# Pinning the order of the casts and subtractions that make the weight forms of a fast matrix product

## The chip, the cores and the metric

The kernel runs on one core of one Trainium2 chip. The metric is the device time of one execution in microseconds (us), the median of several runs. The engines are TensorE (PE, with its weight loads shown as PEld), VectorE (DVE), ScalarE (ACT), GpSimd (POOL) and SyncE (SP). SP, ACT and POOL issue the DMAs.

## The reference

One layer of a decoder trunk on 512 tokens of width 2048, in float32: a norm, a combined projection, two kinds of attention, an output projection, and then the gated MLP in which the change lies:

```python
D_MODEL = 2048; SEQ = 512; D_FF = 5632
def conv_ffn(h, w_up, conv_w, conv_b, w_down):
    u, g = jnp.split(h @ w_up, 2, axis=-1)
    u = lax.conv_general_dilated(
        u, conv_w[:, None, :], window_strides=(1,), padding=((CONV_WIDTH - 1, 0),),
        dimension_numbers=('NWC', 'WIO', 'NWC'), feature_group_count=D_FF) + conv_b
    return (jax.nn.silu(u) * g) @ w_down

x = x + g2 * conv_ffn(h, w_up[l], conv_w[l], conv_b[l], w_down[l])
return rms_norm(x, norm_final)
```

The first product is `h @ w_up`, the second is the one with `w_down` (5632 x 2048).

## The kernel before

A float32 operand is split into two parts that PE takes at its faster rate: a high part, made by a cast on ACT (L215), and a low part, the operand less the high part, made by a subtraction on DVE (L218). `split_to` makes both, and each product of two matrices is three matmuls: high by high, high by low, low by high.

The second product is done block by block with a scheme that needs seven products instead of eight for a matrix cut into 2 x 2 blocks. The 44 feature tiles make five groups of eight and a last group of four, which is done plainly at the end (`Kept`, `last_slots`). A group has two passes, one for each half of the output columns, so there are ten passes, `n` = 0 to 9. In a pass there are seven products, `pos` = 0 to 6, each in two halves of the depth, `p` = 0 and 1. One `pos` and `p` is a slot: 12 matmuls of 128x512 into the output tile `p` (class `Down`).

A pass works on four raw weight blocks a, b, c, d of 128x1024 for each `p`. For `p` = 0 they lie in tiles of their own (`qa`, `qb`, `qc`, `qd`); for `p` = 1 they lie in two shared tiles, `rawca` and `rawbd`. Block a of passes 2, 4, 6 and 8 lies in `rawa`. `dn_cut` makes the weight form of a slot. It splits a block (`cut`, into one of four tiles `wd` that are used in turn), combines blocks in place on DVE for a later position (L1285 c - a, L1290 s = d - c, L1296 s - a, L1308 b - s; s is `qs` or `rawst`), and calls `dn_load`, which has SP load a block of the next pass over the one just used (L1278).

The activations need forms as well, `af`, made once for a group by `act_form` out of the tiles `stage`: four positions of them are made in the second pass of the group before, positions 3 to 6, and three in the first pass of the group itself, positions 0 to 2. They take the subtractions L1261 to L1266 and further splits.

`drive` runs over the slots and calls `split` three slots ahead of the matmuls. Results leave PSUM by a copy on ACT (L1375) and are added up in memory by DMAs of POOL (`total`, L1320).

This is the order in which the program is recorded, and it is not the order in which the engines run it. A scheduler sets the order of every engine's queue from priorities and from its own estimate of when operands are ready. An engine then works through its queue in that order. `tc.keep_in_program_order` adds an order edge from the instruction recorded just before on the same engine, so that the scheduler can't put the pinned instruction ahead of it. Before the change the loads L1278, the sums of POOL and some casts of other parts are pinned; `split_to` and `cut` have an argument `keep` that pins the cast alone.

The first product runs up to about 1640 us of the span (tiles `ux`, `uy`, `uz`); its last slots overlap with the first of the second one. The convolution's vectors `y`, the sums `ut` and `gt` and the modulation row `mod` of its last unit are still on DVE and ACT then.

Of the kernel before, what the change touches and what calls it, by code (L numbers as in the profile page):

```python
# [11 lines left out]
OP = mybir.AluOpType  # L12
# [21 lines left out]
def hybrid_trunk(ctx, tc, xT, cT, wm, bm, nrm, wik, wiq, wi1, sinks, kvn, wuk, wuv, rel, onehot,  # L34
                 wo, wup, cw, cb, wdn, out):
    nc = tc.nc
    act, dve, pe, pool, sp = nc.scalar, nc.vector, nc.tensor, nc.gpsimd, nc.sync
# [176 lines left out]
    def split_to(hi_t, lo_t, full, keep=False):  # L214
        hi = act.copy(hi_t, full)  # L215
        if keep:
            tc.keep_in_program_order(hi)
        dve.tensor_tensor(lo_t, full, hi_t.bitcast(F32), OP.subtract)  # L218
# [809 lines left out]
    def cut(x, name, keep=False):  # L1028

        w = env["px0"].tile([P, 2, 1024], F32R, tag=f"x2_{cut_turn[0] % 4}", name=f"w{name}")  # L1030
        cut_turn[0] += 1
        split_to(w[:, 0], w[:, 1], x, keep)
        return w[:, 0], w[:, 1]
# [201 lines left out]
    def raw_place(tag, p, name, n):  # L1235
        if tag == "a" and n > 1 and n % 2 == 0:
            return down_t["a2"][:, p]
        return down_t[tag] if p else fr_tile(tag, name)
# [32 lines left out]
    def dn_load(n, p, tag):  # L1271
        if n >= 2 * GROUPS:
            return
        g, c = divmod(n, 2)
        t = dn_raw[n, p, tag] = raw_place(tag, p, f"q{tag}{n}_{p}", n)
        k, dq = {"a": (0, c), "b": (1, c), "c": (0, 2 + c), "d": (1, 2 + c)}[tag]
        tc.keep_in_program_order(
            sp.dma_start(t.rearrange("p (a b) -> p a b", a=2), wdn[2 * g + k, dq][:, 2 * p:2 * p + 2]))  # L1278

    def dn_cut(n, pos, p):  # L1280
        a, b, c, d = [dn_raw[n, p, t] for t in "abcd"]
        name = f"d{n}_{pos}_{p}"
        if pos == 0:
            w = cut(a, name)
            dve.tensor_tensor(c, c, a, OP.subtract)  # L1285
            return w
        if pos == 1:
            w = cut(c, name)
            s = dn_raw[n, p, "s"] = raw_place("s", p, f"qs{n}_{p}", n)
            dve.tensor_tensor(s, d, c, OP.subtract)  # L1290
            dn_load(n + 1, p, "c")
            return w
        s = dn_raw[n, p, "s"]
        if pos == 2:
            w = cut(s, name)
            dve.tensor_tensor(a, s, a, OP.subtract)  # L1296
            return w
        if pos == 3:
            w = cut(d, name)
            dn_load(n + 1, p, "d")  # L1300
            return w
        if pos == 4:
            w = cut(a, name)
            dn_load(n + 2 if n else 1, p, "a")
            return w
        if pos == 5:
            w = cut(b, name)
            dve.tensor_tensor(b, b, s, OP.subtract)  # L1308
            return w
        w = cut(b, name)  # L1310
        dn_load(n + 1, p, "b")
        return w

# [17 lines left out]
    class Down:  # L1331
# [9 lines left out]
        def split(self):  # L1341
            if self.w is None:
                g, odd = divmod(self.n, 2)
                if self.p and odd and self.pos > 2 and g + 1 < GROUPS:
                    act_form(g + 1, self.pos - 3)
                elif self.p and not odd and self.pos < 3 and g:
                    act_form(g, self.pos + 4)
                self.w = dn_cut(self.n, self.pos, self.p)
# [458 lines left out]
```

## Time and profile before

| | |
|---|---|
| median of 3 runs | 2110.59 us (2108.61 to 2114.93) |
| the profiled execution | 2113.66 us, span 2111.9 us |
| mean granted TensorE clock | 0.995 |
| DVE busy, whole span | 1711.7 us (81%) |
| ACT busy, whole span | 1181.4 us (56%) |
| second product | 1639.8 to 2043.5 us, 1680 matmuls of 128x512 |

The profile is of one execution. A row of a timeline has the start in us from the start of the span, the length, the engine and line, what is written and read, the count, and in brackets the idle time of the engine before it with what ended it. Buffer numbers are left out of names. A matmul's recorded length overlaps with the next one's, since matmuls are pipelined.

### The profile page before, as it was taken

How to read it: one execution, taken by the hardware profiler on the slowest of the kernel's cores; microseconds unless marked ns; L12 is line 12 of the kernel's file. 1: busy time of each engine (PE TensorE's matmuls, PEld its weight loads, DVE VectorE, ACT ScalarE, POOL GpSimd, SP SyncE). 2: the span in 40 equal slices, each digit the busy share in tenths (PEclk: the TensorE clock that was granted, in tenths of full speed). 3: DMA queues.
4: the chain of work that ended last, by engine and by line, in shares of the span. 5: the costliest groups of instructions: out<-in, count | busy, mean ns of one | idle time of the engine just before them, and what ended most of it. 6: DMA issues, size and time to landing. Idle time of an engine off the chain costs nothing.

```text
span 2111.9 us, 30184 instructions
## 1 busy us (share of the span) xinstructions
PE 2061.8 (98%) x11050; PEld 1705.7 (81%) x11050; DVE 1711.7 (81%) x2484; ACT 1181.4 (56%) x1950; POOL 287.8 (14%) x432
## 2 busy tenths in 40 slices
PE   8999999999999999999999999999999999999997
PEld 4677877777888888888888888888888787778787
DVE  2887889877868778888888888888888987877867
ACT  4324887677833265555455455555555665665655
POOL 0000000011033200121111111111111111111120
PEclk9999999999999999999999999999999999999999
DMA  9883122567699824887777877787787779989992
GB/s 387 271 278 128 56 74 67 163 212 221 198 349 331 264 88 136 214 217 215 207 215 211 214 215 210 213 221 203 211 223 202 248 236 238 239 212 264 211 237 91
DMA packets 148341, 442.98 MB, mean 210 GB/s; under 512 B 17375, under 2 KB 31855, under 8 KB 141408
## 3 DMA queue, kind: packets, MB, share of 16 engines
q1 hardware_dynamic: 89856, 278.13, 39.4%
q0 software_dynamic: 48832, 145.62, 30.2%
q10 hardware_dynamic: 9504, 17.31, 2.2%
q8 instruction: 86, 1.41, 0.3%
q14 instruction: 63, 0.52, 0.1%
HBM read 366.40 MB, written 58.46 MB: 201 GB/s over the span
## 4 chain that ended last, share of the span: by engine, by line
PE 75%; DVE 11%; DMA 5%; issue 4%; ACT 4%; POOL 0%; SPq 0%; DVEq 0%; ACTq 0%; POOLq 0%
PE ux L53 22%; PE uy L53 11%; PE p L53 9%; PE uz L53 5%; PE qip L53 4%; DVE wd L218 2%; DMA rawca<-in_wdn_dram 2%; DVE af L218 1%; PE ckv L53 1%; DMA mraw<-in_wm_dram 1%; PE mrow L53 1%; PE o L53 1%; DVE wk L688 1%; PE mps L53 1%; DVE top L685 1%
## 5 line engine op out<-in xcount | busy, mean ns | idle before, releaser
L53 PE MATMUL p<-wd,af 128*128 128x512 f32 x1680 | 385.7, 390 | 13.3 <-DVE wd L218 12.8
L53 PEld LDWEIGHTS p<-wd,af 128*128 128x128 f32 x1680 | 314.1, 188 | 84.4 <-DVE wd L218 18.6
L53 PE MATMUL ux<-t_up,wu 128*128 128x512 f32 (+1 forms) x1968 | 368.5, 340 | 1.7 <-DVE gt L1176 1.7
L53 PEld LDWEIGHTS ux<-t_up,wu 128*128 128x128 f32 x1968 | 301.0, 188 | 49.4 <-DVE gt L1176 3.7
L53 PE MATMUL uy<-h,wu 128*128 128x512 f32 (+1 forms) x1312 | 244.2, 339 | 0.0
L53 PEld LDWEIGHTS uy<-h,wu 128*128 128x128 f32 x1312 | 200.7, 188 | 30.1
L231 DVE SCALAR_TENSOR_TENSOR macc<-mraw,c_sb,macc 128x512 f32<-128x512 f32 x240 | 179.5, 748 | 11.3 <-DMA mraw<-in_wm_dram 9.2
L218 DVE TENSOR_TENSOR wu<-ra,wu 128x1024 fp32r<-128x1024 f32 x82 | 100.2, 1222 | 62.0 <-ACT wu L215 62.0
L53 PE MATMUL ux<-h,wu 128*128 128x512 f32 (+1 forms) x656 | 128.6, 339 | 0.0
L215 ACT CAST wu<-rb 128x1024 fp32r<-128x1024 f32 x82 | 86.3, 1053 | 64.5 <-issue 31.6
L53 PE MATMUL uz<-h,wu 128*128 128x512 f32 (+1 forms) x656 | 122.3, 339 | 0.0
L215 ACT CAST wu<-ra 128x1024 fp32r<-128x1024 f32 x82 | 86.1, 1051 | 56.9 <-PE uy L53 49.9
L215 ACT CAST wu<-rs 128x1024 fp32r<-128x1024 f32 x41 | 43.2, 1053 | 129.4 <-DVE rs L1102 81.3
L53 PEld LDWEIGHTS ux<-h,wu 128*128 128x128 f32 x656 | 100.5, 188 | 15.2
L53 PEld LDWEIGHTS uz<-h,wu 128*128 128x128 f32 x656 | 100.5, 188 | 15.1
L218 DVE TENSOR_TENSOR wu<-rb,wu 128x1024 fp32r<-128x1024 f32 x82 | 100.2, 1222 | 8.6 <-ACT wu L215 8.6
L1375 ACT COPY ev<-p 128x512 f32<-128x512 f32 x140 | 81.3, 584 | 25.1 <-PE p L53 21.2
L1320 POOL DMA_DIRECT2D total<-ev x62 | 52.7, 855 | 296.1 <-ACT ev L1375 255.4
L218 DVE TENSOR_TENSOR wu<-rd,wu 128x1024 fp32r<-128x1024 f32 x41 | 50.2, 1225 | 52.3 <-ACT wu L215 52.3
L215 ACT CAST wu<-rd 128x1024 fp32r<-128x1024 f32 x41 | 43.1, 1052 | 69.9 <-PE ux L53 68.2
L1177 POOL DMA_DIRECT2D gt<-gt x41 | 35.2, 860 | 337.7 <-DVE gt L1176 283.1
L1074 POOL DMA_DIRECT2D re<-in_wup_dram x40 | 34.5, 862 | 311.1 <-DMA re<-in_wup_dram 271.4
(1697 smaller groups left out, 4590.8 us busy)
## 6 DMA issues: line engine op xcount, KB each, us to landing
mraw<-in_wm_dram POOLq DMA_DIRECT2D x160, 256.0 KB, 5.8
total<-ev POOLq DMA_DIRECT2D x70, 512.0 KB, 8.0
mraw<-in_wm_dram SPq DMA_DIRECT2D x32, 1024.0 KB
mraw<-in_wm_dram POOLq DMA_DIRECT2D x48, 512.0 KB, 6.4
ra<-in_wup_dram SPq DMA_DIRECT2D x41, 512.0 KB
rc<-in_wup_dram SPq DMA_DIRECT2D x41, 512.0 KB
rb<-in_wup_dram SPq DMA_DIRECT2D x41, 512.0 KB
rd<-in_wup_dram SPq DMA_DIRECT2D x41, 512.0 KB
```

Source lines behind the costliest of these rows:

```text
L53: return self.to.matmul(out, w, x, **kw)
L215: hi = act.copy(hi_t, full)
L218: dve.tensor_tensor(lo_t, full, hi_t.bitcast(F32), OP.subtract)
L231: tc.keep_in_program_order(dve.scalar_tensor_tensor(acc, t, cact[:, kt:kt + 1], acc, OP.mult, OP.add))
L685: dve.max(top[b][:, r], cur[b])
L688: dve.match_replace(wk[b], top[b][:, r], cur[b], -3e38)
L1074: tc.keep_in_program_order(pool.dma_start(duo_raw[f, "e"], duo_part(f, "d"), accum_op=OP.add))
L1177: tc.keep_in_program_order(pool.dma_start(g[:, 1], g[:, 2], accum_op=OP.add))
L1320: tc.keep_in_program_order(pool.dma_start(to, x, accum_op=OP.add))
L1375: act.copy(e[:, b], ps)
```

## The change

In `dn_cut` every `cut` gets `keep` = True, so that each cast of a weight form is pinned behind the instruction recorded before it on ACT; and the four in-place subtractions L1285, L1290, L1296 and L1308 are pinned behind the instruction recorded before them on DVE. The low-part subtraction L218 inside `split_to` isn't pinned itself. No instruction is added or removed.

```diff
         if pos == 0:
-            w = cut(a, name)
-            dve.tensor_tensor(c, c, a, OP.subtract)
+            w = cut(a, name, True)
+            tc.keep_in_program_order(dve.tensor_tensor(c, c, a, OP.subtract))
             return w
         if pos == 1:
-            w = cut(c, name)
+            w = cut(c, name, True)
             s = dn_raw[n, p, "s"] = raw_place("s", p, f"qs{n}_{p}", n)
-            dve.tensor_tensor(s, d, c, OP.subtract)
+            tc.keep_in_program_order(dve.tensor_tensor(s, d, c, OP.subtract))
             dn_load(n + 1, p, "c")
             return w
         s = dn_raw[n, p, "s"]
         if pos == 2:
-            w = cut(s, name)
-            dve.tensor_tensor(a, s, a, OP.subtract)
+            w = cut(s, name, True)
+            tc.keep_in_program_order(dve.tensor_tensor(a, s, a, OP.subtract))
             return w
         if pos == 3:
-            w = cut(d, name)
+            w = cut(d, name, True)
             dn_load(n + 1, p, "d")
             return w
         if pos == 4:
-            w = cut(a, name)
+            w = cut(a, name, True)
             dn_load(n + 2 if n else 1, p, "a")
             return w
         if pos == 5:
-            w = cut(b, name)
-            dve.tensor_tensor(b, b, s, OP.subtract)
+            w = cut(b, name, True)
+            tc.keep_in_program_order(dve.tensor_tensor(b, b, s, OP.subtract))
             return w
-        w = cut(b, name)
+        w = cut(b, name, True)
         dn_load(n + 1, p, "b")
         return w
```

How the queues change is shown at three places. In the names a weight form is `wd_`, its position, its `p` and a number of the tile; an activation form is `af_` with its position.

The first is DVE's queue in pass 3, positions 1 to 3. Tiles 16138 to 16215 belong to pass 3; `qc_0_16140` and the `rawca` that is combined with `rawa` are block c of pass 4.

```order
-L218 TENSOR_TENSOR wd_0_1_16116<-rawca,wd_0_1_16116 128x1024
+L218 TENSOR_TENSOR wd_2_1_16194<-rawst,wd_2_1_16194 128x1024
 L1296 TENSOR_TENSOR rawca<-rawst,rawca 128x1024
-L218 TENSOR_TENSOR wd_1_0_16135<-qc_0_15877,wd_1_0_16135 128x1024
-L218 TENSOR_TENSOR wd_1_1_16156<-rawca,wd_1_1_16156 128x1024
-L1285 TENSOR_TENSOR qc_0_16140<-qc_0_16140,rawa_15613 128x1024
-L218 TENSOR_TENSOR wd_2_0_16178<-qs_0_16138,wd_2_0_16178 128x1024
-L218 TENSOR_TENSOR wd_2_1_16194<-rawst,wd_2_1_16194 128x1024
-L1285 TENSOR_TENSOR rawca<-rawca,rawa_15613 128x1024
 L218 TENSOR_TENSOR wd_3_0_16215<-qd_0_15959,wd_3_0_16215 128x1024
```

Before, the two subtractions L1285 for pass 4 stood among the low parts of positions 1 and 2 of pass 3; now they are gone from here, and L1296 for `rawca` stands behind the low part of its own position.

The second is the same queue at the end of pass 3 and the start of pass 4, where `wd_0_0_16374` is the first form of pass 4.

```order
-L1290 TENSOR_TENSOR qs_0_16415<-qd_0_16218,qc_0_16140 128x1024
 L218 TENSOR_TENSOR wd_6_1_16353<-rawbd,wd_6_1_16353 128x1024
 L218 TENSOR_TENSOR wd_0_0_16374<-rawa_15613,wd_0_0_16374 128x1024
-L1290 TENSOR_TENSOR rawst<-rawbd,rawca 128x1024
+L1285 TENSOR_TENSOR qc_0_16140<-qc_0_16140,rawa_15613 128x1024
 L218 TENSOR_TENSOR af_4_16390<-stage_15230,af_4_16390 128x1024
 L218 TENSOR_TENSOR wd_0_1_16393<-rawa_15613,wd_0_1_16393 128x1024
+L1285 TENSOR_TENSOR rawca<-rawca,rawa_15613 128x1024
+L218 TENSOR_TENSOR wd_1_0_16412<-qc_0_16140,wd_1_0_16412 128x1024
+L1290 TENSOR_TENSOR qs_0_16415<-qd_0_16218,qc_0_16140 128x1024
 L218 TENSOR_TENSOR af_4_16390<-stage_15231,af_4_16390 128x1024
```

The subtractions L1285 and L1290 for pass 4 now stand in pass 4, each behind the low part that is recorded before it. The other passes change in the same way.

The third is ACT's queue at the handover from the first product, where `rawst` and `stage` hold activations for pass 0.

```order
 L215 CAST wd_0_0_15266<-qa_0_15179 128x1024
-L215 CAST wd_0_1_15298<-rawca 128x1024
 L215 CAST af_0_15202<-stage_01_15048 128x1024
 L1041 ACTIVATE y_15258<-y_15258 128x512
 L215 CAST af_15291<-stage_11_15050 128x1024
 L1044 DMA actd_1646<-y_15258 128x512
+L215 CAST af_2_15294<-rawst 128x1024
+L215 CAST wd_0_1_15298<-rawca 128x1024
 L215 CAST wd_1_0_15302<-qc_0_15103 128x1024
-L215 CAST af_2_15294<-rawst 128x1024
 L1184 COPY gt_15264<-ux_15128 128x256
```

The cast of the second weight form of pass 0 has moved behind five rows, the last of them the cast of activation form 2. Later on ACT the cast of `wd_4_1` moves behind that of `wd_5_0` in pass 0, and behind that of an activation form in the odd passes 1, 3, 5 and 7; its other rows stay, but for a few evacuations in pass 0. On SP one load of `rawa` moves ahead of a load of `rawca`; POOL's queue stays as it was. PE's queue changes in pass 0 alone, where the matmuls on the high and the low parts of the first forms are put in another order.

## The prediction, made before the result was known

> **What bounds the kernel now.** I read the page first. TensorE (PE) is busy for 98% of the span, so only the gaps that it still has can be won, and I looked for those of the second product (output tile `p`, weight forms `wd`, activation forms `af`).
>
> ```profile
> span 2111.9 us, 30184 instructions
> PE 2061.8 (98%) x11050; PEld 1705.7 (81%) x11050; DVE 1711.7 (81%) x2484; ACT 1181.4 (56%) x1950; POOL 287.8 (14%) x432
> L53 PE MATMUL p<-wd,af 128*128 128x512 f32 x1680 | 385.7, 390 | 13.3 <-DVE wd L218 12.8
> ```
>
> The 1680 matmuls of this product stood idle for 13.3 us, 12.8 of it behind VectorE (DVE) writing a low weight part. The timeline of PE alone (start, length, what, and in brackets the idle time before it) gives the places.
>
> ```profile
> 1643.34 3.09 PE L53 MATMUL ux<-t_up,wu 128*128 128x512 f32 x16 [1.72 <-DVE gt L1176]
> ...
> 1649.09 8.64 PE L53 MATMUL p<-wd,af 128*128 128x512 f32 x36 [1.02 <-DVE wd L218]
> 1658.22 0.50 PE L53 MATMUL p<-wd,af 128*128 128x512 f32 x1 [0.49 <-ACT ev L1375]
> 1659.10 37.96 PE L53 MATMUL p<-wd,af 128*128 128x512 f32 x166 [0.38 <-DVE wd L218]
> 1698.38 81.89 PE L53 MATMUL p<-wd,af 128*128 128x512 f32 x360 [1.32 <-DVE wd L218]
> 1781.86 13.94 PE L53 MATMUL p<-wd,af 128*128 128x512 f32 x60 [1.58 <-DVE wd L218]
> 1796.62 25.01 PE L53 MATMUL p<-wd,af 128*128 128x512 f32 x108 [0.83 <-DVE wd L218]
> 1822.54 38.39 PE L53 MATMUL p<-wd,af 128*128 128x512 f32 x168 [0.91 <-DVE wd L218]
> 1862.60 13.90 PE L53 MATMUL p<-wd,af 128*128 128x512 f32 x60 [1.67 <-DVE wd L218]
> 1877.35 25.01 PE L53 MATMUL p<-wd,af 128*128 128x512 f32 x108 [0.85 <-DVE wd L218]
> 1903.25 51.97 PE L53 MATMUL p<-wd,af 128*128 128x512 f32 x228 [0.89 <-DVE wd L218]
> 1955.99 25.02 PE L53 MATMUL p<-wd,af 128*128 128x512 f32 x108 [0.77 <-DVE wd L218]
> 1983.57 59.91 PE L53 MATMUL p<-wd,af 128*128 128x512 f32 x263 [2.55 <-DVE wd L218]
> ...
> 2098.77 0.35 PE L53 MATMUL rs_1s<-ones,tail 128*128 128x1 f32 x2 [0.22 <-DVE tail L1479]
> ```
>
> There are three small gaps at the handover from the first product, nine from 1698 on, and then none until 2098.77, after the last product: whatever the second product saves, the end should come earlier by as much. Why DVE is late shows in its own timeline ahead of the gap at 1781.86.
>
> ```profile
> 1771.66 1.23 DVE L1285 TENSOR_TENSOR qc<-qc,rawa 128x1024 f32<-128x1024 f32 x1 [5.58 <-DMA qc<-in_wdn_dram]
> 1772.80 1.22 DVE L218 TENSOR_TENSOR wd<-qs,wd 128x1024 fp32r<-128x1024 f32 x1
> ...
> 1779.44 1.23 DVE L1285 TENSOR_TENSOR rawca<-rawca,rawa 128x1024 f32<-128x1024 f32 x1 [4.29 <-issue]
> 1780.58 1.22 DVE L218 TENSOR_TENSOR wd<-qd,wd 128x1024 fp32r<-128x1024 f32 x1
> ```
>
> Both L1285 subtractions belong to the next pass and read blocks that are still in flight. The queue of SP shows when those loads went out, and ScalarE (ACT) shows that the hi part of the form was long there:
>
> ```profile
> 1763.39 0.33 SPq L1278 DMA_DIRECT2D qc<-in_wdn_dram  x1
> 1766.11 0.33 SPq L1278 DMA_DIRECT2D rawca<-in_wdn_dram  x1
> ```
> ```profile
> 1771.93 1.06 ACT L215 CAST wd<-qd 128x1024 fp32r<-128x1024 f32 x1 [1.19 <-PE p L53]
> ```
>
> The loads take 8.3 us (1763.39 to 1771.66) and at most 13.3 us (1766.11 to 1779.44). The cast for wd<-qd was done at 1772.99; its DVE half waited in line behind L1285 until 1780.58 and ended at 1781.80; PE started at 1781.86. So the last wait is a load, held at the head of DVE's queue. The view of waits over 1655 to 2044 (total us, times, longest) says that this is the pattern:
>
> ```profile
> ACT wd L215 <- PE p L53: 69.1, 70, 4.0
> DVE qc L1285 <- DMA qc<-in_wdn_dram: 23.2, 5, 6.8
> ACT af L215 <- DVE stage L1262: 17.8, 4, 6.0
> DVE rawca L1285 <- issue: 15.7, 4, 5.2
> DVE qs L1290 <- DMA qd<-in_wdn_dram: 8.2, 3, 3.1
> DVE rawca L1285 <- DMA rawca<-in_wdn_dram: 7.7, 3, 4.0
> ```
>
> The four DVE rows make 54.8 us of waiting; PE feels only what outlasts its lead.
>
> **The change, part by part.** Nothing is added or removed: 70 pairs of pass and position keep their casts, subtractions and loads.
>
> *The subtractions of DVE.* In the steady passes L1285, L1290 and L1296 move back to the pass that uses them. L1285 for the first half goes about twelve slots later (a slot is 12 matmuls of one weight form). A slot is 2.72 us: row 1698.38 holds 360 matmuls, (81.89 - 0.39) / 359 = 0.227 us each. Twelve slots are 33 us behind the load's issue, for a load that needs 8.3 to 13.3; L1290 comes ten slots (27 us) after its load of `qd`. So the 54.8 us of waits should go, and with them the nine gaps. A break costs the idle time plus what a matmul's record overhangs its successor, 0.39 - 0.227 = 0.16 us:
>
> 1.32 + 1.58 + 0.83 + 0.91 + 1.67 + 0.85 + 0.89 + 0.77 + 2.55 = 11.37 us; with 9 x 0.16 = 1.47, 12.8 us.
>
> Two kinds are in this sum. 1698, 1781, 1822, 1862, 1903 and 1983 follow a late L1285 at once. 1796 and 1877 come 14.8 us after the gap ahead of them, while DVE works off its backlog without a pause, and I take 1955 to be of that kind; with no stall there is no backlog.
>
> *What is late next: DVE in the crowded stretch.* From position 4 of an odd pass to position 2 of the next, DVE must also split the activation forms. In the changed order 30 instructions stand there for 12 slots: 30 x 1.135 us (1771.66 to 1772.80, back to back) = 34.0 us against 32.7 of PE. Before, two of them (L1285) had been done ahead of it. The excess of 1.4 us comes out of the lead: a cast may start when the slot four back has ended, three slots (8.2 us) before its use, and cast plus subtraction take 1.05 + 1.22, so 5.9 us are free. Walking the changed queues through with these durations, the tightest form is done 4 us before PE wants it. Cost taken: nothing. If the cover were gone, PE would wait for what exceeds 5.9 us.
>
> *The casts of ACT.* Most keep their rows. In odd passes the cast for `wd_4_1` now stands behind the form cast that waits for L1262 (17.8 us over four times, longest 6.0, because DVE was late); queued behind it are `wd_5_0` and an evacuation. With DVE on time L1262 ends 0.6 us into a slot and the subtraction of `wd_4_1` is done 4 us ahead of use. Nothing.
>
> *The handover.* Here ACT casts `af_2` before `wd_0_1`, and DVE takes L1180, L1266 and the `af_2` subtraction first.
>
> ```profile
> 1644.53 1.06 ACT L215 CAST af<-rawst 128x1024 fp32r<-128x1024 f32 x1 [0.71 <-DVE rawst L1264]
> ```
> ```profile
> 1644.41 1.22 DVE L218 TENSOR_TENSOR wd<-rawca,wd 128x1024 fp32r<-128x1024 f32 x1
> ...
> 1647.82 1.22 DVE L218 TENSOR_TENSOR wd<-qc,wd 128x1024 fp32r<-128x1024 f32 x1
> ...
> 1657.83 1.22 DVE L218 TENSOR_TENSOR wd<-qs,wd 128x1024 fp32r<-128x1024 f32 x1
> ```
>
> The low half of `wd_0_1` ends at 1648.5 instead of 1645.6, that of `wd_1_0` at 1650.8 instead of 1649.0. PE is reordered to match (hi products first). Following it matmul by matmul, the first 51 are issued by 1659.2; before, the 52nd started at 1659.10 after its gaps. I take 0, between a loss of 2.9 us (the delay of `wd_0_1` in full) and a gain of 1.9 (1.02 + 0.49 + 0.38 all gone).
>
> *SP's queue* at one place: the first `rawa` load of pass 2 is put ahead of `rawca` of pass 1 and of the two `stage` loads.
>
> ```profile
> 1668.98 0.33 SPq L1278 DMA_DIRECT2D rawca<-in_wdn_dram  x1
> ...
> 1678.58 0.80 SPq L1278 DMA_DIRECT2D rawa<-in_wdn_dram  x2
> ```
> ```profile
> 1667.81 0.33 ACTq L1044 DMA_DIRECT2D actd<-y  x1
> ut<-ut POOLq DMA_DIRECT2D x41, 256.0 KB, 3.4
> ```
>
> It waits for the first product's buffers to be free. Their last store, also 256 KB, goes out at 1667.81; at the 3.4 us that a transfer of that size takes on POOL's queue (an estimate) it lands at 1671.2. So `rawca` goes out about 2 us late, and its user has 5.9 us of lead. 0, at worst 3. POOL's queue is unchanged, its transfers following PE's pace.
>
> The sum: 12.8 us off the profiled execution. That one took 2113.66 us for a span of 2111.9, 3.1 above the median 2110.59; taken off the median, **2097.8 us**, say 2098 (0.6%). A change below 0.3% (6.3 us) can't be told from none here.
>
> **A rule against it.** PE also waits behind buffers: in the first of the wait rows the casts themselves wait 69.1 us for PE to free one of four weight tiles. If the gaps came from that, order would not help. The Trainium skill (Perfetto Trace Analysis, Optimization Strategy) says that a gap repeating on the engine that should be saturated can mean that there isn't enough SBUF or PSUM for the next tile. By that rule the time would stay at 2110.6. The rows speak against it: at 1781.86 the cast had been over for 8.9 us when PE went on, so a tile was there.
>
> **The rivals.**
> 1. *Forecast*: all nine gaps go, 2098. Chance 0.60.
> 2. *The backlog gaps stay*, since DVE has more to do in the crowded stretch: 1796, 1877 and 1955 keep 0.83 + 0.85 + 0.77 + 3 x 0.16 = 2.9 us: 2100.7. 0.13.
> 3. *The handover pays* its bound of 2.9 us: 2100.7, with rival 2 2103.6. 0.12.
> 4. *No change*: the gaps are for want of tiles, or the loads are late anyway. For the second the DMA share would have to be at its end:
>
> ```profile
> 1640.00:2044.00 404.00, 389.01 (x1702) 317.08 (x1701) 321.68 (x287) 252.16 (x323) 60.09 (x75) 1.00 0.89 234
> ```
>
>    The last two numbers are the share, 0.89, and 234 GB/s. The same transfers in 391 us make 0.92: room, though little. Time 2110.6, chance 0.08. By the Trainium skill (Perfetto Trace Analysis, Identifying the Most-Contended Engine) bandwidth and not occupancy tells whether DMA binds; the row gives both, and no run so far decides between them.
> 5. *Slower: DVE and ACT in lockstep in the crowded stretch.* Nine times there a cast waits for a DVE result and a DVE subtraction for that cast. If none of the nine casts were covered by another DVE instruction, DVE would idle 9 x 1.05 = 9.5 us, and 34.0 + 9.5 - 32.7 - 5.9 = 4.9 us would reach PE, in four stretches 19.6: 2110.6 + 19.6 - 12.8 = 2117.4. It decides as soon as more than four of nine are bare (4.5 us), and beats the gain at about eight. Against it: in the changed order at least one other subtraction (1.135 us) stands between each such pair. 0.07.
>
> That the change does nothing is ruled out by the order: DVE's queue is another one in every pass.
>
> **Numbers.** Faster by over 0.3% (under 2104.3) hold rivals 1 to 3: 0.85, less 0.02 for several small losses at once: 0.83. Within: 0.10. Slower: 0.07. The range reaches down to all gaps and the handover's 1.9 gone, with the scatter of the runs (some 2 us), 2094, and up to rivals 2 and 3 together, 2104.
>
> **What would show it.** Right: no idle DVE time ahead of L1285, PE without gaps from 1660 to the last product, the handover's length as before, DVE's idle time now behind casts of `wd`. Wrong: gaps <-DVE wd around positions 4 to 2 of odd to even passes (rivals 2, 5), DMA waits in front of L1290 or a cast (4), a gap over 2 us before 1660 (3).

## The result, and the profile after

The changed kernel takes 2098.86 us (median of 4, 2098.56 to 2101.0), the kernel before 2112.76 (median of 4, 2108.61 to 2115.35): a ratio of 0.9937, with a 95% interval from 0.9921 to 0.9953. The forecast was 2098. The profiled execution of the changed kernel took 2099.02 us, for a span of 2097.3.

The page of the changed kernel, in the rows that were shown of the kernel before:

```profile
span 2097.3 us, 30196 instructions
PE 2056.4 (98%) x11050; PEld 1705.2 (81%) x11050; DVE 1714.3 (82%) x2484; ACT 1183.9 (56%) x1950; POOL 287.8 (14%) x432
L53 PE MATMUL p<-wd,af 128*128 128x512 f32 x1680 | 382.2, 389 | 1.7 <-DVE wd L218 1.1
```

The idle time of the second product's matmuls fell from 13.3 to 1.7 us. Their busy time fell too, by 3.5 us, though they are as many; this is taken up below. The timeline of PE from the end of the first product (start, length, what, idle time before it):

```profile
1642.54 3.09 PE L53 MATMUL ux<-t_up,wu 128*128 128x512 f32 x16 [1.95 <-DVE gt L1176]
...
1646.72 0.73 PE L53 MATMUL p<-wd,af 128*128 128x512 f32 x2 [0.44 <-ACT wd L215]
1647.75 1.43 PE L53 MATMUL p<-wd,af 128*128 128x512 f32 x5 [0.30 <-DVE wd L218]
1650.02 377.94 PE L53 MATMUL p<-wd,af 128*128 128x512 f32 x1666 [0.84 <-DVE wd L218]
...
2044.34 0.44 PE L57 MATMUL cT<-identr,ct 128*128 128x128 f32 x2 [0.92 <-DMA ct<-total]
```

From 1650.02 on, 1666 matmuls run as one piece: all nine gaps are gone. Small ones are left at the handover, and a new one of 0.92 us stands in the tail, ahead of the transposes `cT`. The view of waits over 1655 to 2032 (total us, times, longest) says what the other engines now wait for:

```profile
DVE wd L218 <- ACT wd L215: 53.5, 66, 3.0
...
ACT wd L215 <- PE p L53: 36.9, 45, 1.1
...
ACT af L215 <- DVE stage L1262: 3.4, 4, 0.9
```

No row of DVE waiting for a load is left; the 54.8 us are gone. Part of that idle time is still there, but now behind casts, whose forms PE needs later: 53.5 us, against the row of the kernel before (1655 to 2044)

```profile
DVE wd L218 <- ACT wd L215: 20.8, 22, 1.5
```

Where the span's 14.6 us come from, by these rows and those of before:

- Ahead of the handover, where nothing was changed, the last row of `ux` stands 0.80 us earlier. That is taken as scatter.
- The handover: the run from 1650.02 begins with the 15th matmul of the product. A matmul takes (377.94 - 0.39) / 1665 = 0.2268 us on average. By the starts of the single matmuls in the trace the 52nd starts at 1658.56; before, at 1659.10. That is 0.54 earlier, so 0.26 was lost against the 0.80.
- From the 52nd matmul to the end of the last: before, 1983.57 + 59.91 - 1659.10 = 384.38 us; now 1650.02 + 377.94 - 1658.56 = 369.40. 14.98 us are won here.
- The tail gives back 0.92. In all, 0.80 - 0.26 + 14.98 - 0.92 = 14.6.

### The profile page after: what moved, and what is told of

Its sections match the earlier page's. It is cut to its first block, busy times and chain, and to the rows that moved or that the text cites. A ratio compares the mean times of both kernels' runs of the same rounds, so it can differ in the third digit from the quotient of the medians.

```text
span 2097.3 us, 30196 instructions
## 1 busy us (share of the span) xinstructions
PE 2056.4 (98%) x11050; PEld 1705.2 (81%) x11050; DVE 1714.3 (82%) x2484; ACT 1183.9 (56%) x1950; POOL 287.8 (14%) x432
## 4 chain that ended last, share of the span: by engine, by line
PE 81%; DVE 6%; issue 5%; DMA 4%; ACT 3%; POOL 0%; SPq 0%; DVEq 0%; POOLq 0%; ACTq 0%
PE ux L53 22%; PE p L53 17%; PE uy L53 11%; PE uz L53 5%; PE qip L53 4%; DMA mraw<-in_wm_dram 2%; DMA total<-ev 1%; PE ckv L53 1%; PE mrow L53 1%; DVE wk L688 1%; DVE top L685 1%; PE mps L53 1%; DVE sa L803 1%; PE o L53 1%; PE wo2ps L53 1%
## 5 line engine op out<-in xcount | busy, mean ns | idle before, releaser
L218 DVE TENSOR_TENSOR wu<-ra,wu 128x1024 fp32r<-128x1024 f32 x82 | 100.1, 1221 | 61.6 <-ACT wu L215 61.6
L218 DVE TENSOR_TENSOR wu<-rb,wu 128x1024 fp32r<-128x1024 f32 x82 | 100.1, 1221 | 8.2 <-ACT wu L215 8.2
L218 DVE TENSOR_TENSOR wu<-rd,wu 128x1024 fp32r<-128x1024 f32 x41 | 50.2, 1225 | 51.8 <-ACT wu L215 51.8
```

## The experiments

**Which pins do it.** Two theories. The one of the prediction: what cost time was L1285 waiting in DVE's queue for a load in flight, so its pins alone bring the whole gain. The rival: the casts come in a better order, or it takes all pins together. The first kernel has the four pins of DVE alone (L1285 and L1290 are shown, L1296 and L1308 are edited in the same way).

```
-            dve.tensor_tensor(c, c, a, OP.subtract)
+            tc.keep_in_program_order(dve.tensor_tensor(c, c, a, OP.subtract))
...
-            dve.tensor_tensor(s, d, c, OP.subtract)
+            tc.keep_in_program_order(dve.tensor_tensor(s, d, c, OP.subtract))
...
```

> Only the four in-place subtractions on DVE are pinned, the casts on ACT are not. Theory (subtractions of the next pass stood early in DVE's queue and waited there for loads in flight): the nine gaps of PE after 1660 us are gone, time 2099 within 3 us, ratio to the kernel before 0.9935. Rival (the pinned casts bring the gain): within 3 us of the kernel before, about 2111.

Measured: 2096.78 us, ratio 0.9928 (0.9913 to 0.9942): the whole gain. The second has the seven pins of the casts alone (one of the seven is shown).

```
-            w = cut(a, name)
+            w = cut(a, name, True)
...
```

> Only the casts on ACT are pinned, DVE's subtractions are free and L1285, L1290 stay early as before. Theory: the nine gaps stay, about 2111 (within 3 us of the kernel before), ratio 1.000. Rival (the casts bring the gain): about 2099.

Measured: 2113.06 us, ratio 1.0002 (0.999 to 1.0014): nothing. Its page has the gaps, its waits have the loads, as before:

```profile
L53 PE MATMUL p<-wd,af 128*128 128x512 f32 x1680 | 387.6, 392 | 12.8 <-DVE wd L218 12.2
```
```profile
DVE qc L1285 <- DMA qc<-in_wdn_dram: 16.4, 4, 6.1
DVE rawca L1285 <- issue: 12.2, 4, 3.6
```

The third pins one line, L1285; the queues of PE, ACT, SP and POOL are then the same as before, and the handover with them.

```
-            dve.tensor_tensor(c, c, a, OP.subtract)
+            tc.keep_in_program_order(dve.tensor_tensor(c, c, a, OP.subtract))
```

> One of the eleven pins: L1285 alone. The queues of PE, ACT, SP and POOL are row for row those of the kernel before; on DVE L1285 moves back into its own pass and pulls L1290 along, since that reads its result. Theory: all of the gain, 2099 to 2101, no wait of L1285 for a load, no gap of PE after 1660. Rival (the gain needs the casts, or the new order on PE or SP at the handover): no gain, or less than half of it, 2105 to 2111.

Measured: 2099.34 us, ratio 0.9937 (0.9923 to 0.9951), and one piece of 1629 matmuls behind the handover:

```profile
1658.60 369.54 PE L53 MATMUL p<-wd,af 128*128 128x512 f32 x1629 [0.40 <-DVE wd L218]
```

One pin is enough. It moves L1285, and L1290, which reads its result, moves along; what L1290's 8.2 us of waits for `qd` cost by themselves was not tried. The fourth kernel is the changed one with that pin taken off and the other ten left.

```
-            tc.keep_in_program_order(dve.tensor_tensor(c, c, a, OP.subtract))
+            dve.tensor_tensor(c, c, a, OP.subtract)
```

> Ten of the eleven pins, L1285 is free: the scheduler puts it one to three rows later than before (behind wd_2_0 and wd_3_0 of the pass ahead), still about nine slots early. Theory: the wait of L1285 for its load shrinks by one or two slots (2.7 to 5.4 us of 5 to 7), so that some of the gaps stay: 2101 to 2108. Rival (the other pins bring the gain): 2099, no gaps.

Measured: 2102.82 us, ratio 0.9953 (0.994 to 0.9965). The other pins alone push L1285 one to three rows back, and the loads have landed for the most part; two rows of waits are left, 12.4 + 4.3 = 16.7 us in place of the 46.6 of L1285 before, and 2.8 us of idle time at the matmuls. These pins bring 9.8 us, the pin at L1285 alone 13.3: most of the gain comes as soon as L1285 stands a few rows further back.

```profile
DVE rawca L1285 <- DMA rawca<-in_wdn_dram: 12.4, 5, 3.5
DVE qc L1285 <- DMA qc<-in_wdn_dram: 4.3, 3, 3.5
```
```profile
L53 PE MATMUL p<-wd,af 128*128 128x512 f32 x1680 | 384.3, 390 | 2.8 <-DVE wd L218 2.2
```

**The early place, or the load?** Moving L1285 changes two things, where DVE spends its time and what it waits for. This kernel keeps the early place and takes the loads away.

```
             dve.tensor_tensor(s, d, c, OP.subtract)
-            dn_load(n + 1, p, "c")
+            dn_raw[n + 1, p, "c"] = c
```

> Before with no pin, but the 18 loads of block c after pass 0 left out: L1285 then works again and again on the block that lies there (another sum is computed). On DVE L1285 stands as early as before, in three places one row earlier still. Theory (what costs is a load in flight at the head of DVE's queue, not the early place): no DMA wait ahead of L1285 or L1290, no gap of PE from 1660 to the last product, 2098 to 2100 us. Rival (the early place costs by itself, because each L1285 puts the low parts behind it back by 1.135 us into a crowded queue): the gaps stay, 2108 to 2113.

Measured: 2100.22 us (2095.46 to 2101.39), ratio 0.995 (0.993 to 0.997). L1285 stands as early as before, and PE runs through:

```profile
1655.13 369.58 PE L53 MATMUL p<-wd,af 128*128 128x512 f32 x1629 [0.42 <-DVE wd L218]
```

So it was the loads. Two short waits of L1285 for `rawa`, 2.9 and 0.4 us in pass 1, are left, though none was expected; PE does not feel them. This also tells what stood behind a row that the profile had left without a cause: the 15.7 us of `rawca L1285 <- issue` before are gone with the loads of block c, though those of `rawa`, which it reads too in two of the four places, are still there.

**How much lead there is in the crowded stretch.** The prediction took nothing for DVE's 34.0 us of work in 32.7, because the tightest form would be done 4 us early. These kernels are the changed one with more work in the second half of that stretch, positions 0 to 2 of the even passes, and look for the end of the lead there. Three more subtractions a stretch:

```
                 self.w = dn_cut(self.n, self.pos, self.p)
+                for _ in range(1 * (self.p and self.n in (2, 4, 6, 8) and self.pos < 3)):
+                    tc.keep_in_program_order(dve.tensor_tensor(*[down_t["spare"]] * 3, OP.subtract))
```

> As the kernel with six, but three in a stretch, one behind the second form of each position: 3.4 us. Theory (some 4 us of lead): nothing, 2098 to 2100. Rival A: 4 x 3.4 = 13.6, 2112. Rival B: nothing; the pair of runs tells theory from both.

Measured: 2099.54 us, ratio 0.9943 (0.9922 to 0.9964): free. Six more (without the condition on `self.p`):

> The changed kernel with six more DVE subtractions of 128x1024 (of one unused tile from itself, 1.135 us each) in each of four crowded stretches, one behind every form of positions 0 to 2 of passes 2, 4, 6 and 8: 6.8 us of DVE work a stretch. Theory (the tightest form is done some 4 us before PE wants it): what exceeds the lead reaches PE, 6.8 - 4 = 2.8 us and the 0.16 of a break, in four stretches 12: 2109 to 2112. Rival A (DVE is at its end there already): all of it, 4 x 6.8 = 27: 2126. Rival B (much more lead than worked out): nothing, 2099.

Measured: 2106.67 us, ratio 0.9974 (0.9964 to 0.9984). Against the 2099.54 of the kernel with three more that is 7.1 us, 1.8 in each stretch: between the rivals, but less than the 12 expected. PE's timeline around the first stretch:

```profile
1649.42 88.17 PE L53 MATMUL p<-wd,af 128*128 128x512 f32 x386 [0.85 <-DVE wd L218]
1738.24 2.83 PE L53 MATMUL p<-wd,af 128*128 128x512 f32 x11 [0.64 <-DVE wd L218]
1741.64 73.96 PE L53 MATMUL p<-wd,af 128*128 128x512 f32 x325 [0.57 <-DVE wd L218]
```

The place is right: the gap ahead of 1738.24 ends with the low part of the second form of position 2, in DVE's timeline of that kernel

```profile
1736.95 1.23 DVE L218 TENSOR_TENSOR wd<-rawst,wd 128x1024 fp32r<-128x1024 f32 x1
```

which ends at 1738.18. The lead in the changed kernel can be read directly. This form is the 34th of the product; PE comes to it with matmul 397, in the trace at 1736.76. DVE's timeline of the changed kernel has its low part in the row

```profile
1731.53 1.22 DVE L218 TENSOR_TENSOR wd<-rawst,wd 128x1024 fp32r<-128x1024 f32 x1
```

which ends at 1732.75, 4.0 us before, and the other forms of positions 0 to 3 are done 4.2 to 5.6 before. So the 4 us were right for this part of the stretch (for the part ahead of it they were not, as the next section shows), and the expected price was still wrong. PE's queue in the kernel with six more says why:

```
 L53 MATMUL p_1_0_15902<-wd_2_1_15940,af_2_15770 128x512 [waits Activation_49]
 L53 MATMUL p_1_1_15903<-wd_2_1_15940,af_2_15770 128x512
 L53 MATMUL p_5_0_15945<-wd_3_0_15962,af_2_15770 128x512 [waits Activation_49]
 L53 MATMUL p_5_1_15946<-wd_3_0_15962,af_2_15770 128x512 [waits Activation_49]
 L53 MATMUL p_1_0_15902<-wd_2_1_15940,af_2_15770 128x512 [waits DVE_49]
```

In the changed kernel the second matmul of the form waits for DVE; here three more matmuls, which need only high parts, stand ahead of that wait, as the scheduler has laid out PE's queue anew. Four of 0.2268 are 0.9 us, so the lead is 4.9; five added subtractions stand ahead of this form, 5 x 1.135 = 5.7 us; 0.8 is short, and the row shows 0.64 + 0.16 for the break. The sixth stands ahead of the next form and makes the second gap, 0.57 + 0.16. Twelve more a stretch (a 2 in place of the 1):

> As the kernel with six more DVE subtractions in each crowded stretch, but two behind every form: 13.6 us a stretch. Six cost 7.1 us in four stretches, so about 6.8 - 1.8 = 5.0 us of a stretch were covered. If the lead is one cover used once a stretch: 4 x (13.6 - 5.0) = 34, 2134. Rival (DVE catches up between the forms, so that the cover counts again): under 2125.

Measured: 2131.4 us (2130.02 to 2135.6), ratio 1.01 (1.0084 to 1.0116), where the changed kernel took 2098.04 on the same chip: 33.4 us, 8.3 a stretch, so 13.6 - 8.3 = 5.3 were covered. The lead is used up once a stretch; past it DVE's work costs nearly its full time: 6.8 us more a stretch than with six subtractions cost 6.6 us more.

**Tiles.** The rival of the prediction that gaps are for want of weight tiles is tried by taking one of the four away from pass 2 on, and making forms two slots ahead instead of three (three further calls of `drive` are edited like the one shown).

```
-        w = env["px0"].tile([P, 2, 1024], F32R, tag=f"x2_{cut_turn[0] % 4}", name=f"w{name}")
+        w = env["px0"].tile([P, 2, 1024], F32R, tag=f"x2_{(cut_turn[0] + 2) % 3 if name > 'd2' and name[0] == 'd' else cut_turn[0] % 4}", name=f"w{name}")
...
-        drive(slots, at, at + 28)
+        drive(slots, at, at + 28, ahead=2)
...
```

> The changed kernel with three weight tiles in turn instead of four from pass 2 on, and forms made two slots ahead instead of three: each cast has 2.72 us less. Theory (a lead of 4 us in the tightest place, and tiles were never what lacked): 4 - 2.7 = 1.3 us are left, 2098 to 2102. Rival (weight tiles bound the casts, which wait 36.9 us for PE to free one): a gap of up to 2.7 us at each of the four crowded stretches or more often, 2110 and above.

Measured: 2099.5 us, ratio 0.9947 (0.9928 to 0.9965). The casts wait for PE far longer, and PE does not notice:

```profile
ACT wd L215 <- PE p L53: 66.5, 76, 1.2
```
```profile
1652.32 378.30 PE L53 MATMUL p<-wd,af 128*128 128x512 f32 x1666 [0.85 <-DVE wd L218]
```

A wait for a tile that has its lead costs nothing, here 66.5 us of it against 36.9. The rule of the Trainium skill (Perfetto Trace Analysis, Optimization Strategy), that repeating gaps can mean too little memory for the next tile, names a possibility that this case's runs exclude: with the same four tiles the pin at L1285 takes the gaps away, and with a tile fewer they do not come back. The same edit on the kernel before:

> The kernel before, without pins, with three weight tiles and forms made two slots ahead from pass 2 on, as was done to the changed kernel. Theory (a load in flight at the head of DVE's queue, of which the lead hides a part; the lead is now 2.72 us less): the six gaps behind a late L1285 grow by 2.7 each, the other three by up to as much: 16 to 24 us, 2128 to 2137. Rival (the early place costs only DVE's time, not its lead): as before, 2112.

Measured: 2115.02 us (2109.88 to 2120.51), ratio 1.001 (0.9998 to 1.0022). The expected 16 to 24 us did not come; the rival's number did, but not for its reason. The scheduler, with forms made later, laid DVE's queue out otherwise: five steady gaps are left in place of nine, and they are larger, 1.13 to 2.31 us.

```profile
1779.04 78.10 PE L53 MATMUL p<-wd,af 128*128 128x512 f32 x336 [1.91 <-DVE wd L218]
1859.44 76.46 PE L53 MATMUL p<-wd,af 128*128 128x512 f32 x336 [2.31 <-DVE wd L218]
```

L1285 still waits for its load, but in a pass like that of 1776 only the first of the two does. The experiment changed two things at once and does not settle the price of lost lead in the kernel before.

**The pins of the casts, and the tail.** The changed kernel had small gaps at the handover and a wait of 0.92 us ahead of `ct`; the profile with DVE's pins alone had no wait there, and its median was 2 us lower. So the casts' pins were suspected. Both kernels once more, side by side and without an edit:

> The changed kernel itself once more, to stand beside the one with the DVE pins alone on the same chip: 2098 to 2100.

> The four pins of the DVE subtractions alone, once more. If the pins of the casts cost something (small gaps at the handover, 0.7 us, and the wait ahead of ct in the tail, 0.9): about 1.6 us below the changed kernel, 2096 to 2098. If they don't: the same time within 1 us.

Measured: 2098.04 us for the changed kernel and 2097.9 for DVE's pins alone, ratios 0.9935 (0.9922 to 0.9948) and 0.9933 (0.9921 to 0.9946). The wait ahead of `ct` was 0.29 and 0.83 us this time, the other way round:

```profile
2043.15 0.44 PE L57 MATMUL cT<-identr,ct 128*128 128x128 f32 x2 [0.29 <-DMA ct<-total]
```
```profile
2043.96 0.44 PE L57 MATMUL cT<-identr,ct 128*128 128x128 f32 x2 [0.83 <-DMA ct<-total]
```

So the casts' pins cost no time and bring none, no version here is measurably faster than the changed kernel, and one pin, at L1285, does what its eleven do. The wait in the tail varies from execution to execution of one kernel; it was between 0 and 1.69 us in the kernels of this study that are faster than before. What sets it (the sums `total` that `ct` is loaded from are added up by POOL's transfers) wasn't tried.

## Why the prediction was right, point by point

- **The cause** was right, and is shown, not only argued: the pin at L1285 (which takes L1290 along) brings the gain, the ten others without it bring less, the casts bring none, and the early place without a load in flight costs nothing.
- **The nine gaps** went, those of the backlog (1796, 1877, 1955) too, so rival 2 fell. But the step "11.37 + 1.47 = 12.8 us" was too small: the stage from the 52nd matmul on won 14.98. The term that was too small is the price of a break. The rows of PE's timeline hide breaks that are shorter than the overhang of a matmul's record. Before, the row from 1796.62 holds 108 matmuls in 25.01 us; at the undisturbed 0.2268 they take 107 x 0.2268 + 0.39 = 24.66, so 0.35 is lost inside the row. The nine rows from 1698 on hide 1.8 us in this way, and the row of 166 ahead of them 0.15: 12.8 + 1.8 + 0.15 = 14.8. The starts of the single matmuls in the trace show where most of it is: in each of the nine rows the second matmul starts some 0.337 us behind the first in place of 0.227, 1.0 us in all, and in the rows from 1796, 1877 and 1955 two more starts each are 0.1 late, 0.6 us. With the 1.5 of overhangs these 1.95 are nearly all of the 3.5 us by which the busy time fell.
- **"Whatever the second product saves, the end should come earlier by as much"** held but for the 0.92 us of the wait ahead of `ct`, which the profiled execution of the kernel before did not have.
- **The number** 2098 owes something to luck: two misses cancel. The gain was about 2 us larger than summed, and the median of before is 2112.19 to 2112.78 in the result and the experiments, about 2 more than the 2110.59 that it was taken from.
- **The crowded stretch** cost nothing, but "the tightest form is done 4 us before PE wants it" was not so. 4.0 us is the lead in the even passes, where three more subtractions fitted in and six did not. The tightest form of the stretch stands earlier, in the odd passes, at the second half of position 5:

```profile
1705.28 1.22 DVE L218 TENSOR_TENSOR wd<-rawca,wd 128x1024 fp32r<-128x1024 f32 x1
1710.95 1.22 DVE L218 TENSOR_TENSOR wd<-rawbd,wd 128x1024 fp32r<-128x1024 f32 x1
```

  It is done at 1712.17, and PE starts it at 1714.99, 2.8 us later; so it is in passes 1, 3, 5 and 7. There the work that could still be added for nothing was not measured. Rival 5, lockstep, fell: DVE's 53.5 us behind casts never reach PE.
- **The casts of ACT**: nothing, as said. The wait for L1262 fell from 17.8 to 3.4 us, once DVE no longer waited for loads. But L1262 ends 1.6 us into a slot and not 0.6 (1779.17, where the slot starts at 1777.56), and `wd_4_1` is done 3.1 us ahead of use and not 4: the first of the two rows ends at 1706.50, and PE starts that form at 1709.56.
- **The handover**: 0 forecast, 0.26 lost, so rival 3 fell.
- **SP's queue**: the delay came out as forecast, but not for the reason given. In the changed kernel's queue of SP `rawca` goes out behind `rawa`, at 1670.41; with 0.80 for the earlier start that is 2.2 us later than the 1668.98 of before (about 2 forecast), and nobody waits for it. Yet `rawa` did not wait for the last store of the first product to land: it went out at 1666.95, just ahead of that store.

```profile
1666.95 0.41 SPq L1278 DMA_DIRECT2D rawa<-in_wdn_dram  x1
1670.41 0.33 SPq L1278 DMA_DIRECT2D rawca<-in_wdn_dram  x1
```
```profile
1667.01 0.34 ACTq L1044 DMA_DIRECT2D actd<-y  x1
```
```profile
1669.17 1.21 DVE L218 TENSOR_TENSOR wd<-rawca,wd 128x1024 fp32r<-128x1024 f32 x1
```

  `rawca` went out when DVE had read the old block, at 1670.38. This is the low part of `wd_4_1` of pass 0, which now stands behind that of `wd_5_0`; before, it started at 1667.70, ended at 1668.92, and the load went out at 1668.98. PE starts this form at 1671.48, so its lead was only 1.1 us, a place that the prediction did not work out.

- **The loads are not at their end** (rival 4). The stage's row of the changed kernel, and that of the kernel without block c's loads:

```profile
1640.00:2031.00 391.00, 387.32 (x1719) 319.78 (x1718) 325.53 (x290) 256.45 (x325) 60.97 (x76) 1.00 0.93 242
```
```profile
1640.00:2030.00 390.00, 388.07 (x1732) 321.02 (x1732) 323.98 (x288) 254.91 (x323) 60.42 (x76) 1.00 0.86 218
```

The share of the DMA engines rose from 0.89 to 0.93 (0.92 was worked out), the rate from 234 to 242 GB/s, and PE ran through. With the loads of block c gone the share is 0.86 and the time no better. That is what the Trainium skill (Perfetto Trace Analysis, Identifying the Most-Contended Engine) warns of: a high share of busy DMA engines is no proof that they bind.

## What to carry to other kernels

In a queue that runs in order, work for a later stage that stands early can cost little by its own time and much by what it waits for, as here: look for waits for loads on an engine that feeds the bound one, and ask what stands behind them. Put such work where its operands have long landed, here one line, and check that the place it goes to still has lead; that lead can be measured by adding idle work until the time moves, but only for the place where the work is added. When gaps are summed, compare the length of a run of instructions with the same count from an undisturbed run, or the small breaks inside it are missed.

## What the runs showed of the hardware that was not expected

A load of 512 KB on SP's queue was waited for up to 13.3 us after its issue in the kernel before (1766.11 to 1779.44); in the same kernel with three weight tiles, one issued at 1771.12 was used without a wait by 1778.90, 7.8 us.

```profile
1771.12 0.33 SPq L1278 DMA_DIRECT2D rawca<-in_wdn_dram  x1
```
```profile
1778.90 1.22 DVE L1285 TENSOR_TENSOR rawca<-rawca,rawa 128x1024 f32<-128x1024 f32 x1
```

What differs is a load of 1024 KB on the same queue. In the kernel before it goes out between the loads of `qc` and `rawca`, in the kernel with three tiles ahead of both:

```profile
1763.88 0.38 SPq L1701 DMA_DIRECT2D x2b<-x2d  x1
```
```profile
1760.89 0.45 SPq L1701 DMA_DIRECT2D x2b<-x2d  x1
```

So it is in passes 3, 5 and 7: L1285 starts 13.3, 13.4 and 11.4 us after the issue of its `rawca` in the one kernel, and 7.8, 8.2 and 7.3 us in the other. That the large load ahead makes the small one late is likely by this, but was not tried by itself.

And the wait ahead of `ct` was 0.92 and 0.29 us in two executions of one and the same kernel, while the medians of the changed kernel and of the one with DVE's pins alone lie 0.14 us apart.
